# Gates kept as logits, an ungated attention projection, and another spacing of the attention's steps in a hybrid decoder block

## Chip, cores and metric

The kernel runs on one core of one Trainium2 chip. The metric is the device time of one execution in microseconds; the median of several executions is given.

## What is computed

One decoder block over 2048 tokens of width 1024, all in float32. A normalised input is projected to 7680 columns, and two branches run beside each other: a gated depthwise convolution over 31 taps with layernorm, and sliding-window attention (16 heads over 4 key-value heads, window 128, one sink a head). Each has a SiLU gate of its own, an output projection, and a sigmoid gate by which the two are merged.

```python
h = rmsnorm(x, norm_g[l])
proj = jnp.einsum("bsd,de->bse", h, w_in[l])
glu_in, conv_gate, q, k, v, attn_gate, merge_logits = jnp.split(proj, SPLIT_POINTS, axis=-1)
c = conformer_conv(glu_in, conv_dw_w[l], conv_dw_b[l], conv_ln_g[l], conv_ln_b[l])
y_conv = jnp.einsum("bsc,cd->bsd", c * jax.nn.silu(conv_gate), w_conv_out[l])
...
a = sliding_window_attention(q, k, v, attn_sinks[l])
y_attn = jnp.einsum("bsa,ad->bsd", a * jax.nn.silu(attn_gate), w_attn_out[l])
gates = jax.nn.sigmoid(merge_logits)
g_conv, g_attn = jnp.split(gates, 2, axis=-1)
merged = g_conv * y_conv + g_attn * y_attn
x = x + jnp.einsum("bsd,de->bse", merged, w_out[l])
return rmsnorm(x, final_norm_g)
```

## The kernel before

The tokens are taken in two sweeps of 1024. In a sweep nothing is transposed back: projections come out with 128 columns of weights on the partitions and 1024 tokens beside them, as two halves of 512. Every such item has 48 matmuls of 128x128 on 128x512, since each float32 operand is split into a high and a low part and three products are made (hi·hi, hi·lo, lo·hi). TensorE's order is the order of the code. The other engines' orders are made by a scheduler that takes instructions by readiness and priority.

The items of a sweep, in this order: k, v and q with rope (tiles ra, rb, hq); 32 gate items, ag (attention's gate), cg (convolution's gate), ma and mc (the two merge gates); among all these 8 pairs of items gb and ga (the convolution's input), each of which starts a convolution on VectorE (L513 and L520, 31 steps into acc, then cv); then ya, the attention's output projection, 8 items; yc, the convolution's, 8 items; and o, the last projection, 16 items.

A gate's values go from PSUM through an activation to a buffer of the ring t2k (five buffers of 128x512) and by DMA to HBM. They come back by `load_gate` where they are multiplied: cg with the layernormed convolution, giving u (`gated`, L927), ma in ya's evacuation (L999, into mp), mc in yc's (L1022, and GpSimd adds mp in L1023, giving mT by a split).

A clock of nominal microseconds, `Line`, places smaller work between the matmuls. It counts 3 x 0.2275 for three matmuls. `late` holds chains with a due time: a chain is a generator that yields the time its matmuls take and the time until its next step. `soon` holds single operations, one of which goes out at each count, and `bg` a queue of operations at a fixed interval, above all the convolutions' steps.

The attention is such a set of chains, 32 units a sweep (4 key-value heads, 8 blocks of 128 queries), one started each ATT_EVERY = 13.8, while the gate items run. A unit has three steps on TensorE: the scores (sc, eight small matmuls, L766); after LAT[0] four transposes of the softmax (tpp, L796); after LAT[1] the product with v (ov, six matmuls, L820). Between sc and tpp stand ScalarE's copy, VectorE's masked copy (L782) and maximum (L785), four exponentials (L787), a reciprocal and four scalings (L791). Between tpp and ov stand ScalarE's copy (L805) and VectorE's split (L253) into pt, and GpSimd's selection (L809) into pc. Behind ov come ScalarE's copies (L828) and VectorE's adds (L830), the gate (L831) and a split, and the result is stored to HBM, from where ya's operand aT is loaded. The scores of two halves, tpp and ov take turns in three PSUM banks (pool tp_ps). The projections have three banks of their own (mm_ps).

`high_priority(offset)` moves instructions ahead by so many places for the scheduler: 60 for an evacuation (PRIO), 120 for a step of a chain, 1200 where `front()` stands.

The pieces of q are stored to HBM by `drain`, a chain that issues one store each 2.0; `flush` issues what is left, before the buffers are used again and before the attention starts. SP, one queue, issues all DMAs, the weights' among them (L267 the raw weight; L270 its low part, kept in HBM by sweep 0 for sweep 1; L728 and L732 a unit's q and k).

Of the kernel before, what the change touches and what calls it, by code (L numbers as in the profile page):

```python
# [15 lines left out]
AF = mybir.ActivationFunctionType  # L16
ALU = mybir.AluOpType
# [5 lines left out]
KC = D // P  # L23
# [3 lines left out]
TH = 512  # L27
# [6 lines left out]
C_GLU_A, C_GLU_B, C_CGATE, C_Q, C_K, C_V, C_AGATE, C_MC, C_MA = (  # L34
    0, 1024, 2048, 3072, 4096, 4352, 4608, 5632, 6656)
# [9 lines left out]
ROPE_EVERY = 3.2  # L45
CONV_EVERY = 2.4
ATT_EVERY = 13.8
LAT = (27.0, 7.0)
PRIO = 60
SCALE = HD ** -0.5  # L50

# [2 lines left out]
def hybrid_block(ctx: ExitStack, tc: tile.TileContext, x, xt, par_d, w_in, w_conv, sinks, w_attn, w_out,  # L54
                 fin_g, rope_t, out):
    nc = tc.nc
    pe, act, dve, pool = nc.tensor, nc.scalar, nc.vector, nc.gpsimd
# [13 lines left out]
    def f(ap):  # L71
        return ap.bitcast(F32)
# [8 lines left out]
    def slot(tag, shape, dt, name):  # L81
        n = int(np.prod(shape[1:]))
        full = 1024 + P if tag in WIDE else 1024
        t = slots.tile([P, full], dt, tag=tag, name=name)
        v = t[:, 0:n]
        if len(shape) == 3:
            v = v.rearrange("p (a b) -> p a b", b=shape[2])
        elif len(shape) == 4:
            v = v.rearrange("p (a b c) -> p a b c", b=shape[2], c=shape[3])
        return v  # L90

    def t2k(name, dt=F32):
        return work.tile([P, TH], dt, tag="t2k", name=name, bufs=5)
# [75 lines left out]
    class Line:  # L169
# [27 lines left out]

        def step(self, chain, ok):

            with tc.high_priority(offset=2 * PRIO):  # L200
                got = next(chain, None)
            if got is not None:
                self.t += got[0]
                self.late.append((self.t + got[1], chain, ok))
# [40 lines left out]
    line = Line()  # L245
# [77 lines left out]
    def put_split(dst, src32, lo_eng):  # L323
        act.copy(dst[:, 0, :], src32)
        split_lo(dst[:, 1, :], src32, dst[:, 0, :], lo_eng)
# [171 lines left out]
    def sweep(s):  # L497
# [61 lines left out]
        def gate_item(kind, col, func, e):  # L559
            def ev(half, ps):  # L560
                g = t2k(f"{kind}{s}_{e}_{half}")
                act.activation(out=g, in_=ps, func=func)

                def store():
                    nc.sync.dma_start(out=spill[kind][s * KC + e, :, half * TH:(half + 1) * TH], in_=g)
                    if half == 1:
                        stored.add((kind, e))

                line.soon.append(store)

            return project(w_in[col // P + e], h_rhs, f"{kind}{s}_{e}", ev)

        def load_gate(kind, e, half):
            g = t2k(f"l{kind}{s}_{e}_{half}")
            nc.sync.dma_start(out=g, in_=spill[kind][s * KC + e, :, half * TH:(half + 1) * TH])
            return g


# [31 lines left out]
            t0 = s * T + half * TH  # L610
            nc.sync.dma_start(out=d_k[:, i, :, t0:t0 + TH].rearrange("a p t -> p a t"), in_=f(hl))

        pair, pend = {}, deque()

        def drain():
            while pend:
                pend.popleft()()
                yield 0.0, 2.0

        def flush():  # L620
            while pend:
                pend.popleft()()

        def store_q(r):
            def store(i, half, src):
                n = 2 * i + half
                if r % 2 == 0:
                    flush()
                    pair[n] = [slot(tags[n], [P, NB, 2, HD], F32R, f"hq{s}_{r}_{n}_{tags[n]}")
                               for tags in (AT[7:11], C[2:6])]  # L630
                hi, lo = (t[:, :, r % 2, :] for t in pair[n])
                src = src.rearrange("p (b t) -> p b t", t=HD)
                act.activation(out=hi, in_=src, func=AF.Copy, scale=SCALE)
                dve.scalar_tensor_tensor(out=lo, in0=src, scalar=SCALE, in1=f(hi), op0=ALU.mult,
                                         op1=ALU.subtract)
                if r % 2:
                    b0 = s * 2 * NB + NB * half
                    idle = not pend
                    for a in range(2):
                        pend.append(lambda a=a: nc.sync.dma_start(  # L640
                            out=d_q[a, i, :, b0:b0 + NB, r // 2, :],
                            in_=f(pair[n][a]).rearrange("p b h t -> p b (h t)")))
                    if idle:
                        line.start(drain())

            return store
# [104 lines left out]
        def attention(n):  # L751
# [38 lines left out]
            for h in range(GQ):  # L790
                act.activation(out=sb[:, h, :], in_=sb[:, h, :], func=AF.Copy, scale=rinv[:, h:h + 1])  # L791
            yield 0.90, LAT[0]

# [13 lines left out]
            for a in range(2):  # L807
                at = slice(a * HD, (a + 1) * HD)
                pool.affine_select(out=pc[at], in_=f(pt[0:HD, a]), pattern=[[0, 2 * GQ], [1, HD]],  # L809
                                   compare_op=ALU.is_ge, fill=0.0, base=0, channel_multiplier=-1)  # L810
            yield 0.44, LAT[1]

# [110 lines left out]
        aT, uT = [[None] * KC, [None] * KC], []  # L923

        def gated(dst, kind, e, half, other):
            g = load_gate(kind, e, half)
            dve.tensor_tensor(out=g, in0=g, in1=other(), op=ALU.mult)  # L927
            put_split(dst, g, dve)

# [25 lines left out]
            uT.extend(make_tiles(HT, h, f"uT{s}_") for h in range(2))  # L955

        gates = [gate_item("ag", C_AGATE, AF.Silu, e) for e in range(KC)]
        gates += [gate_item("cg", C_CGATE, AF.Silu, e) for e in range(KC)]
        gates += [gate_item("ma", C_MA, AF.Sigmoid, e) for e in range(KC)]
        gates += [gate_item("mc", C_MC, AF.Sigmoid, e) for e in range(KC)]  # L960
        line.every = ROPE_EVERY

        def ahead(item, work):
# [27 lines left out]
        mp = {}  # L991

        def ya_item(e, first):
            def ev(half, ps):
                if half == 0:
                    line.until(lambda: ("u", e, 1) in stored)
                    mp[e] = slot(C[e], [P, T], F32, f"mp{s}_{e}")
                g = load_gate("ma", e, half)
                dve.tensor_tensor(out=mp[e][:, half * TH:(half + 1) * TH], in0=ps, in1=g, op=ALU.mult)  # L999

            prefetch, blocks, _ = project(w_attn[e], lambda k, half: aT[half][k],
                                       f"ya{s}_{e}", ev)
            if not first:
                return prefetch, blocks

            def first_blocks():
                start_u()
                if None in aT[0] + aT[1]:
                    line.finish()
                yield from blocks()  # L1010

            return prefetch, first_blocks
# [4 lines left out]
        def yc_item(e):  # L1017
            def ev(half, ps):
                if not mT:
                    mT.extend(make_tiles(AT, h, f"mT{s}_") for h in range(2))  # L1020
                g = load_gate("mc", e, half)
                dve.tensor_tensor(out=g, in0=ps, in1=g, op=ALU.mult)  # L1022
                pool.tensor_tensor(out=g, in0=g, in1=mp[e][:, half * TH:(half + 1) * TH], op=ALU.add)  # L1023
                put_split(mT[half][e], g, dve)

            return project(w_conv[e], lambda k, half: uT[half][k], f"yc{s}_{e}", ev)
# [191 lines left out]
```

## Time and profile before

| | |
|---|---|
| median of 3 runs | 2040.08 us (2039.16 to 2041.83) |
| the profiled execution | 2039.39 us, of which the span is 2037.7 us |
| granted clock, mean | 0.995 |
| TensorE busy | 1989.0 us, 9264 matmuls |
| VectorE, ScalarE, GpSimd busy | 1312.7, 1002.2, 431.0 us |

The span runs from the first to the last instruction. Busy time of TensorE counts matmuls that overlap once, and a stalled or half-clocked matmul counts as busy too. In a row of a timeline stand start, duration, engine, line, operation, tiles written and read, the number of merged instructions, and in brackets how long the engine was idle and what ended that.

### The profile page before, as it was taken

Reading aid. Unit: us, or ns where it says so; the run is one execution under the profiler, and the core shown is the slowest. Engines: PE = TensorE matmul, PEld = TensorE weight load, DVE = VectorE, ACT = ScalarE, POOL = GpSimd, SP = SyncE. Lnnn points to the kernel's source line nnn. Section 1 sums busy time; section 2 is a strip of 40 time slices with the busy share of each in tenths; the row PEclk is TensorE's granted clock in tenths of the full one; section 3 lists DMA queues with packets and bytes.
Section 4 is the critical chain, followed back from the end, with each engine's and each line's share of the span. In section 5 each row is a group of like instructions: output and inputs, shape, how many; then the busy total and the mean of one; then the engine's idle time right before and its main releaser. Section 6 shows DMA issues by size and latency. Waiting matters only on the chain.

```text
span 2037.7 us, 27935 instructions
## 1 busy us (share of the span) xinstructions
PE 1989.0 (98%) x9264; PEld 1658.1 (81%) x9264; DVE 1312.7 (64%) x1737; ACT 1002.2 (49%) x2193; POOL 431.0 (21%) x462
## 2 busy tenths in 40 slices
PE   8999999999999999999999989999999999999998
PEld 7888888878787888888888878887888788888887
DVE  7999769878984176123857758688878824441324
ACT  7322576567667454123523125776666674621222
POOL 0444233233333222241011020111111110001200
PEclk9999999999999999999999999999999999999999
DMA  8655665555566857445647564565556578574432
GB/s 302 211 166 194 214 188 168 180 179 177 163 190 205 262 188 240 140 160 207 217 144 228 176 184 148 180 191 173 174 181 192 178 222 271 178 232 149 147 117 83
DMA packets 302785, 382.04 MB, mean 187 GB/s; under 512 B 30000, under 2 KB 160944, under 8 KB 302640
## 3 DMA queue, kind: packets, MB, share of 16 engines
q1 hardware_dynamic: 302640, 380.25, 57.5%
q8 instruction: 74, 1.21, 0.2%
q14 instruction: 71, 0.58, 0.1%
HBM read 252.20 MB, written 127.93 MB: 187 GB/s over the span
## 4 chain that ended last, share of the span: by engine, by line
PE 56%; DVE 20%; ACT 6%; issue 5%; DMA 2%; POOL 2%; SPq 1%; POOLq 0%; ACTq 0%; DVEq 0%
DVE acc L520 12%; PE o L1140 9%; PE mm_yc L291 9%; PE mm_mc L291 8%; PE mm_ya L291 7%; PE mm_ga L291 6%; PE mm_ma L291 5%; PE mm_gb L291 3%; PE mm_cg L291 2%; PE mm_ag L291 1%; ACT ss L787 1%; DVE st L785 1%; PE mm_q_a L291 1%; PE mm_v L291 1%; ACT L787 1%
## 5 line engine op out<-in xcount | busy, mean ns | idle before, releaser
L520 DVE SCALAR_TENSOR_TENSOR acc<-glu,par,acc 128x1024 f32<-128x1024 f32 x464 | 596.2, 1285 | 7.6
L1140 PE MATMUL o<-wo,mT 128*128 128x512 f32 x768 | 174.8, 389 | 0.0
L1140 PEld LDWEIGHTS o<-wo,mT 128*128 128x128 f32 x768 | 144.1, 188 | 30.0
L291 PE MATMUL mm_ma<-hT,whi_ma 128*128 128x512 f32 x512 | 160.8, 395 | 0.0
L291 PE MATMUL mm_cg<-hT,whi_cg 128*128 128x512 f32 x512 | 159.6, 393 | 0.0
L291 PE MATMUL mm_ag<-hT,whi_ag 128*128 128x512 f32 x512 | 159.6, 393 | 0.0
L291 PE MATMUL mm_mc<-hT,whi_mc 128*128 128x512 f32 x512 | 158.4, 390 | 0.0
L291 PE MATMUL mm_ya<-aT,whi_ya 128*128 128x512 f32 x512 | 157.6, 389 | 0.5 <-DVE mp L999 0.5
L291 PE MATMUL mm_yc<-uT,whi_yc 128*128 128x512 f32 x512 | 157.4, 389 | 0.0
L787 ACT ACT_TABLE_LOAD x61 | 78.3, 1283 | 148.3 <-DVE st L785 148.2
L809 POOL TENSOR_SCALAR_AFFINE_SELECT pc<-pt 64x512 fp32r<-64x512 f32 x128 | 84.5, 660 | 272.1 <-ACT pt L805 229.8
L291 PE MATMUL mm_ga<-hT,whi_ga 128*128 128x512 f32 x448 | 141.6, 398 | 0.0
L291 PE MATMUL mm_gb<-hT,whi_gb 128*128 128x512 f32 x448 | 140.1, 394 | 0.3 <-DVE rb_q__1_1662 L598 0.3
L830 DVE TENSOR_TENSOR ss<-ov,ss 64x256 f32<-64x256 f32 x128 | 53.8, 420 | 116.0 <-ACT ss L828 114.5
L291 PEld LDWEIGHTS mm_ya<-aT,whi_ya 128*128 128x128 f32 x512 | 96.0, 188 | 20.7 <-DVE mp L999 0.9
L291 PEld LDWEIGHTS mm_yc<-uT,whi_yc 128*128 128x128 f32 x512 | 96.1, 188 | 19.9
L291 PEld LDWEIGHTS mm_mc<-hT,whi_mc 128*128 128x128 f32 x512 | 95.4, 188 | 19.4
L291 PEld LDWEIGHTS mm_ma<-hT,whi_ma 128*128 128x128 f32 x512 | 94.8, 189 | 18.6
L291 PEld LDWEIGHTS mm_ag<-hT,whi_ag 128*128 128x128 f32 x512 | 94.5, 188 | 18.4
L291 PEld LDWEIGHTS mm_cg<-hT,whi_cg 128*128 128x128 f32 x512 | 93.9, 188 | 18.0
L787 ACT ACTIVATE ss<-ss,st 128x129 f32<-128x129 f32 x256 | 100.2, 394 | 16.9 <-DVE st L785 16.1
L291 PE MATMUL mm_ma<-hT,wlo_ma 128*128 128x512 f32 x256 | 100.4, 392 | 0.0
(445 smaller groups left out, 4296.1 us busy)
## 6 DMA issues: line engine op xcount, KB each, us to landing
qk<-d_q SPq DMA_DIRECT2D x256, 64.0 KB, 2.6
d_a<-ss SPq DMA_DIRECT2D x128, 128.0 KB, 2.6
aT<-d_a SPq DMA_DIRECT2D x32, 512.0 KB, 5.8
qk<-d_k SPq DMA_DIRECT2D x240, 64.0 KB, 2.1
d_q<-hq_c SPq DMA_DIRECT2D x16, 512.0 KB, 4.9
raw_ag<-in_w_in_dram SPq DMA_DIRECT2D x32, 256.0 KB, 3.4
d_ag<-ag SPq DMA_DIRECT2D x32, 256.0 KB, 2.2
pc<-d_ag SPq DMA_DIRECT2D x64, 128.0 KB, 2.7
```

Source lines behind the costliest of these rows:

```text
L291: pe.matmul(out=ps, lhsT=a, rhs=b, start=(k == 0 and i == 0), stop=(k == KC - 1 and i == 2))
L520: dve.scalar_tensor_tensor(out=to, in0=glu[c][:, j:j + T], scalar=tap(c, j), in1=acc[c], op0=ALU.mult, op1=ALU.add)
L785: dve.tensor_reduce(out=ngm, in_=ext, axis=AX.X, op=ALU.max, negate=True)
L787: act.activation(out=ext[:, h, :], in_=ext[:, h, :], func=AF.Exp, bias=ngm[:, h:h + 1], accum_out=den[:, h:h + 1])
L809: pool.affine_select(out=pc[at], in_=f(pt[0:HD, a]), pattern=[[0, 2 * GQ], [1, HD]], compare_op=ALU.is_ge, fill=0.0, base=0, channel_multi ...
L830: dve.tensor_tensor(out=to[r], in0=ovp[rows[r][0], :, r], in1=to[r], op=ALU.add)
L1140: pe.matmul(out=ps, lhsT=a[:, c0:c0 + P], rhs=r, start=(k == 0 and i == 0), stop=(k == KC - 1 and i == 2))
```

## The change

cg, ma and mc are stored as they come from the projection (a copy), and `load_gate` activates them in place, behind the load. ya's evacuation becomes a copy by ScalarE; yc's loads both merge gates, VectorE multiplies mp by ma's gate there, and GpSimd adds. LAT goes from (27, 7) to (19, 16), a step's priority from 120 to 1200 places. `drain` waits 4.0 before its first store, and then hands the stores to `soon`.

```diff
-LAT = (27.0, 7.0)
+LAT = (19.0, 16.0)
...
-            with tc.high_priority(offset=2 * PRIO):
+            with tc.high_priority(offset=20 * PRIO):
                 got = next(chain, None)
...
-                act.activation(out=g, in_=ps, func=func)
+                if func is None:
+                    act.copy(g, ps)
+                else:
+                    act.activation(out=g, in_=ps, func=func)
...
-        def load_gate(kind, e, half):
+        def load_gate(kind, func, e, half):
             g = t2k(f"l{kind}{s}_{e}_{half}")
             nc.sync.dma_start(out=g, in_=spill[kind][s * KC + e, :, half * TH:(half + 1) * TH])
+            act.activation(out=g, in_=g, func=func)
             return g
...
         def drain():
+            draining[0] = True
+            yield 0.0, 4.0
             while pend:
-                pend.popleft()()
+                line.soon.append(pend.popleft())
                 yield 0.0, 2.0
+            draining[0] = False
 
         def flush():
-            while pend:
-                pend.popleft()()
+            for ops in (line.soon, pend):
+                while ops:
+                    ops.popleft()()
...
-                    idle = not pend
+                    idle = not draining[0]
...
-            g = load_gate(kind, e, half)
+            g = load_gate(kind, AF.Silu, e, half)
...
-        gates += [gate_item("cg", C_CGATE, AF.Silu, e) for e in range(KC)]
-        gates += [gate_item("ma", C_MA, AF.Sigmoid, e) for e in range(KC)]
-        gates += [gate_item("mc", C_MC, AF.Sigmoid, e) for e in range(KC)]
+        gates += [gate_item("cg", C_CGATE, None, e) for e in range(KC)]
+        gates += [gate_item("ma", C_MA, None, e) for e in range(KC)]
+        gates += [gate_item("mc", C_MC, None, e) for e in range(KC)]
...
-                g = load_gate("ma", e, half)
-                dve.tensor_tensor(out=mp[e][:, half * TH:(half + 1) * TH], in0=ps, in1=g, op=ALU.mult)
+                act.copy(mp[e][:, half * TH:(half + 1) * TH], ps)
...
-                g = load_gate("mc", e, half)
+                ga, g = (load_gate(kind, AF.Sigmoid, e, half) for kind in ("ma", "mc"))
+                dve.tensor_tensor(out=ga, in0=mp[e][:, half * TH:(half + 1) * TH], in1=ga, op=ALU.mult)
                 dve.tensor_tensor(out=g, in0=ps, in1=g, op=ALU.mult)
-                pool.tensor_tensor(out=g, in0=g, in1=mp[e][:, half * TH:(half + 1) * TH], op=ALU.add)
+                pool.tensor_tensor(out=g, in0=g, in1=ga, op=ALU.add)
                 put_split(mT[half][e], g, dve)
```

What this makes of the engines' orders is seen at three places. The lines of the changed kernel are 8 further down from `drain` on (L766 is L774 there, L796 L804, L820 L828, L830 L838, L728 L736), 3 before it. A name is tile, sweep's own numbers (head and block for the attention) and a buffer number.

The first is TensorE in sweep 0, late in the attention. Before, the scores of unit 3_3 were followed at once by the transposes of unit 3_1, two units older:

```order
L291 MATMUL mm_ma_30_5734<-hT_0_4_456,whi_ma_31_5585 128x512 x2
L291 MATMUL mm_ma_30_5734<-hT_0_4_456,wlo_ma_31_5586 128x512
L766 MATMUL sc_3_3_0_5762<-qk_27_5607 128x192 x4
L766 MATMUL sc_3_3_1_5767<-qk_27_5607 128x192 x4
L796 MATMUL tpp_3_1_5790<-ident_r,ss_3_1_5477 128x128 x4
L291 MATMUL mm_ma_30_5734<-hT_0_5_457,whi_ma_31_5585 128x512 x2
L291 MATMUL mm_ma_30_5734<-hT_0_5_457,wlo_ma_31_5586 128x512
```

Now the same scores are followed by 24 matmuls of the gate, and then by the transposes of unit 3_2, one unit older, with ov of unit 3_1 another 12 matmuls behind:

```order
L804 MATMUL tpp_3_2_5830<-ident_r,ss_3_2_5638 128x128 x4
L291 MATMUL mm_ma_31_5815<-hT_1_4_543,whi_ma_31_5598 128x512 x2
L291 MATMUL mm_ma_31_5815<-hT_1_4_543,wlo_ma_31_5599 128x512
L291 MATMUL mm_ma_31_5815<-hT_1_5_544,whi_ma_31_5598 128x512 x2
L291 MATMUL mm_ma_31_5815<-hT_1_5_544,wlo_ma_31_5599 128x512
L291 MATMUL mm_ma_31_5815<-hT_1_6_545,whi_ma_31_5598 128x512 x2
L291 MATMUL mm_ma_31_5815<-hT_1_6_545,wlo_ma_31_5599 128x512
L291 MATMUL mm_ma_31_5815<-hT_1_7_546,whi_ma_31_5598 128x512 x2
L291 MATMUL mm_ma_31_5815<-hT_1_7_546,wlo_ma_31_5599 128x512
L828 MATMUL ov_3_1_5859<-pt_3_1_5695,vt_0_716 128x256 x2
```

So tpp and ov of one unit moved apart, and sc and tpp of one unit together.

The second is VectorE at the same place, in the last convolution of sweep 0 (acc_7). Before, seven of its steps stood between the split of pt of unit 3_1 and that unit's adds:

```order
L253 TENSOR_TENSOR pt_3_1_5797<-tpp_3_1_5790,pt_3_1_5797 128x512
L785 TENSOR_REDUCE st_3_3_5778<-ss_3_3_5772 128x4
L520 SCALAR_TENSOR_TENSOR acc_7_5977<-glu_7_5255,par,acc_7_5977 128x1024 x3
L789 RECIPROCAL st_3_3_5778<-st_3_3_5778 128x4
L520 SCALAR_TENSOR_TENSOR acc_7_5977<-glu_7_5255,par,acc_7_5977 128x1024 x4
L830 TENSOR_TENSOR ss_3_1_5477<-ov_3_1_5847,ss_3_1_5477 64x256 x2
```

Now the split of the next unit's pt comes first, behind the reciprocal and one step:

```order
L793 TENSOR_REDUCE st_3_3_5785<-ss_3_3_5779 128x4
L520 SCALAR_TENSOR_TENSOR acc_7_5986<-glu_7_5267,par,acc_7_5986 128x1024 x2
L797 RECIPROCAL st_3_3_5785<-st_3_3_5785 128x4
L520 SCALAR_TENSOR_TENSOR acc_7_5986<-glu_7_5267,par,acc_7_5986 128x1024
L253 TENSOR_TENSOR pt_3_2_5837<-tpp_3_2_5830,pt_3_2_5837 128x512
L520 SCALAR_TENSOR_TENSOR acc_7_5986<-glu_7_5267,par,acc_7_5986 128x1024 x2
L838 TENSOR_TENSOR ss_3_1_5490<-ov_3_1_5859,ss_3_1_5490 64x256 x2
```

The convolution's steps are as many as before, and stand between other instructions of the attention.

The third is SP in sweep 1, where the attention starts. Before, the last of eight stores of q (hq), a unit's q and k and then the two halves of the weight wlo_ga:

```order
L640 DMA d_q<-hq_2_3_a_10418 128x8x128
L640 DMA d_q<-hq_2_3_c_10419 128x8x128
L728 DMA qk_0_10651<-d_q 32x512 x4
L732 DMA qk_0_10651<-d_k 32x2x256 x3
L270 DMA wlo_ga_20_10583<-d_lo 128x512
L270 DMA wlo_ga_21_10589<-d_lo 128x512
```

Now the weight's halves stand among the stores, and five stores come later:

```order
L648 DMA d_q<-hq_2_0_h_10438 128x8x128
L270 DMA wlo_ga_20_10644<-d_lo 128x512
L740 DMA qk_1_10828<-d_k 32x2x256 x2
L648 DMA d_q<-hq_2_3_a_10482 128x8x128
L648 DMA d_q<-hq_2_3_c_10483 128x8x128
L736 DMA qk_0_10715<-d_q 32x512
L736 DMA qk_1_10828<-d_q 32x512
L740 DMA qk_1_10828<-d_k 32x2x256 x2
L270 DMA wlo_ga_21_10650<-d_lo 128x512
L648 DMA d_q<-hq_2_0_c_10439 128x8x128
```

The weight moved ahead of most of the stores of q.

More of the change, by code (lines that the diff above doesn't have):

```diff
@@ L611, in store_k @@
             nc.sync.dma_start(out=d_k[:, i, :, t0:t0 + TH].rearrange("a p t -> p a t"), in_=f(hl))
-        pair, pend = {}, deque()
+        pair, pend, draining = {}, deque(), [False]
         def drain():
+            draining[0] = True
+            yield 0.0, 4.0
             while pend:
-                pend.popleft()()
+                line.soon.append(pend.popleft())
                 yield 0.0, 2.0
+            draining[0] = False
         def flush():
-            while pend:
-                pend.popleft()()
+            for ops in (line.soon, pend):
+                while ops:
+                    ops.popleft()()
         def store_q(r):
```

## The prediction

> **What bounds the kernel now.** I read the page first: who is busy, and what the chain that ended last is made of.
>
> ```profile
> span 2037.7 us, 27935 instructions
> PE 1989.0 (98%) x9264; PEld 1658.1 (81%) x9264; DVE 1312.7 (64%) x1737; ACT 1002.2 (49%) x2193; POOL 431.0 (21%) x462
> ...
> PE 56%; DVE 20%; ACT 6%; issue 5%; DMA 2%; POOL 2%; SPq 1%; POOLq 0%; ACTq 0%; DVEq 0%
> ```
>
> TensorE (PE) is the bound, and the change leaves its 9264 matmuls alone; it moves some among each other. So the change is worth what it does to TensorE's idle time and to its clock, and nothing else. VectorE (DVE) holds a fifth of the chain, so it must be what TensorE waits for in places. The view of waits, for PE alone, says which:
>
> ```profile
> PE tpp L796 <- DVE ss L830: 19.7, 21, 3.1
> PE ov L820 <- POOL pc L809: 7.9, 7, 2.2
> PE mm_gb L291 <- ACT u_c L361: 5.5, 1, 5.5
> PE mm_ga L291 <- DMA wlo_ga<-d_lo: 5.4, 1, 5.4
> PE tpp L796 <- ACT ss L791: 1.1, 2, 0.8
> PE mm_q_b L291 <- DMA wlo_q_b<-d_lo: 0.8, 1, 0.8
> PE ov L820 <- DVE pt L253: 0.6, 1, 0.6
> PE mm_ya L291 <- DVE mp L999: 0.5, 1, 0.5
> ```
>
> The columns are total, times, longest. The transposes of the softmax (tpp) and the product with v (ov) wait 19.7 + 7.9 + 1.1 + 0.6 = 29.3 us over 64 attention units. One weight at the start of sweep 1's gates costs 5.4. The 5.5 at mm_gb is the kernel's opening, which stays. After four of these waits the granted clock fell to a half; these are windows laid on those stretches (length, then PE, PEld, DVE, ACT and POOL busy, granted clock, DMA share, GB/s):
>
> ```profile
> 338.71:342.13 3.42, 3.42 (x10) 2.66 (x10) 3.39 (x6) 2.27 (x6) 0.76 (x2) 0.50 0.69 218
> 618.61:622.02 3.41, 3.41 (x10) 2.63 (x9) 3.41 (x4) 1.16 (x3) 1.73 (x1) 0.50 0.39 113
> 1212.53:1219.35 6.82, 4.85 (x11) 3.84 (x12) 0.00 (x0) 0.00 (x0) 0.00 (x0) 0.50 0.80 232
> 1424.15:1427.57 3.42, 3.42 (x10) 2.65 (x9) 0.50 (x2) 3.36 (x9) 0.00 (x0) 0.50 0.46 130
> ```
>
> At half clock, half of the busy time is lost: 3 x 3.42 / 2 = 5.1 us in the attention, and 4.85 / 2 = 2.4 at the weight. All that the change can win is thus 29.3 + 5.4 + 5.1 + 2.4 = 42.2 us, with 1.3 more at q_b and ya.
>
> **The spacing (LAT).** How long a place in TensorE's queue is from another, I count in matmuls:
>
> ```profile
> 1020.72 10.88 PE mm_gb L291 x48
> ```
>
> One costs 10.88 / 48 = 0.227 us. Before, tpp of unit n stood right behind the scores of unit n+2, and 33 matmuls (with its own, 7.9 us) ahead of ov of unit n; from that ov to the next tpp were 5.7 us. Small results share three PSUM banks in turn, so a tpp needs the bank of the ov just before it: 5.7 us for ScalarE's copies (L828) and VectorE's adds (L830). Now tpp of unit n+1 stands 24 matmuls (6.3 us with the scores) behind the scores of n+2, and ov of unit n 12 matmuls further. A unit's period without waits is about 13.65 us (some 51 projection matmuls, 11.6, and about 2.1 for its own 18 small ones), so the new distances are: ov to the tpp that takes its bank 10.5 us (was 5.7); tpp to its own ov 13.65 + 3.1 = 16.8 (was 7.9); scores to their tpp 13.65 + 6.3 = 19.9 (was 28); and tpp to the second scores that take its bank 7.8 (was 13.2). Two distances grow, two shrink.
>
> The shrunk one of the softmax has a worst case in the unit whose scores start at 540.47:
>
> ```profile
> 540.47 1.03 PE L766 MATMUL sc<-qk 128*128 128x192 f32 x8
> ...
> 557.17 1.28 ACT L791 ACTIVATE ss<-ss,st 128x128 f32<-128x128 f32 x4
> ```
>
> That is 18.0 us from the scores' start to the last scaling, inside 19.9, and I found none longer among the 64. GpSimd's pc, which ov waited for, gets 16.8 us where 7.9 fell short by 2.2 at most. What is late next is the other shrunk one: the bank of tpp, freed by VectorE's split of pt (L253). It hangs on VectorE's lag in a convolution, seen best in the last one of sweep 0:
>
> ```profile
> 569.39 0.39 PE L291 MATMUL mm_ga<-hT,wlo_ga 128*128 128x512 f32 x1
> 570.10 0.69 DVE L547 TENSOR_TENSOR glu<-mm_ga,glu 128x512 f32<-128x512 f32 x1
> ...
> 578.83 5.26 DVE L520 SCALAR_TENSOR_TENSOR acc<-glu,par,acc 128x1024 f32<-128x1024 f32 x4
> ...
> 608.52 0.38 PE L820 MATMUL ov<-pc,va 128*128 128x256 f32 x1 [0.59 <-POOL pc L809]
> 613.23 1.03 PE L766 MATMUL sc<-qk 128*128 128x192 f32 x8
> 616.40 0.85 DVE L830 TENSOR_TENSOR ss<-ov,ss 64x256 f32<-64x256 f32 x2
> 617.39 0.63 PE L796 MATMUL tpp<-ident_r,ss 128*128 128x128 f32 x4 [3.13 <-DVE ss L830]
> ```
>
> When the gate's multiply (L547) frees a convolution, its 31 steps of 1.29 us stand in VectorE's queue between the attention's, ten to a unit: 12.9 us, and with the unit's own eleven instructions that is more than the period. The lag grows from unit to unit until the convolution ends. From 570.10 to 617.25 VectorE works without a pause, 47.2 us, and TensorE pays the 3.13. In the new order, fewer steps stand ahead of the split that counts: from L547 to the third pt split 25 convolution steps instead of 28 up to that L830, and one pair of L830 (0.85) less, so 47.2 - 3 x 1.29 - 0.85 = 42.5 us, ending at 612.6 on this clock. The second half of these scores starts at 613.23 + 0.45 = 613.7, less the wait of 0.59 ahead of it that goes: 613.1. That is a tie within one convolution step, where before TensorE lost more than 3 us. The same count for all twelve convolutions gives 24.6 us of lateness before, against 20.8 measured at tpp, and 8.9 after, 3.5 of it in the first units of sweep 1. I take 7 us of new waits, at sc. The ends are 0 (each tie holds) and 21 (VectorE's lateness stays as it is, and only changes its place).
>
> **Priority, logits, activations.** With 20 instead of 2 times 60 for each step, a unit's instructions move ahead of evacuations and convolution steps in the queues of ScalarE, VectorE and SP. TensorE's projections have three banks, so an evacuation may come two halves, 2 x 24 x 0.227 = 10.9 us, late; a unit's ScalarE work is far below that. I cost it at nothing; if that cover went, a step of 0.6 us would show for each evacuation. A unit's DMAs move with it, but ss lives as long as before (ov stands 36.7 us behind its scores, 36 before) against the four periods, 54.6, until its buffer is wanted. The activations:
>
> ```profile
> L787 ACT ACT_TABLE_LOAD x61 | 78.3, 1283 | 148.3 <-DVE st L785 148.2
> L562 ACT ACT_TABLE_LOAD x55 | 70.6, 1283 | 3.1 <-DMA d_mc<-mc 1.5 <-issue 0.7
> L562 ACT ACTIVATE cg<-mm_cg 128x512 f32<-128x512 f32 x32 | 19.2, 598 | 0.4
> ```
>
> The order shows 31 and 17 table loads on these two lines, 68 fewer: 87 us of ScalarE. What is added is 96 activations at the load and 32 copies of ya, 128 x 0.6 = 77 us. ScalarE is at half load, so neither is on the path by itself; the shorter softmax is a help that I leave in the tie above.
>
> **ya and yc.** In sweep 0 the u steps (L927, now with a Silu ahead) stand between the normalisation and ya's copies.
>
> ```profile
> 757.61 0.61 PE L291 MATMUL mm_ya<-aT,whi_ya 128*128 128x512 f32 x2
> 760.06 6.92 ACT L896 ACTIVATE cv<-cv,par 128x1024 f32<-128x1024 f32 x6
> ```
>
> Down ScalarE's new order from 760.06 to the weights of ya's third item, with 1.15 for an apply and 0.6 for the rest, I count 18 us, 778.4, and 1.3 for GpSimd's low half; TensorE gets there at 757.6 + 96 x 0.227 = 779.4. That is another tie: the 0.5 of mp goes, and I put 1 us there, between 0 and one half, 5.4. In yc each half now loads two gates into a ring of five buffers, so the load for half i+2 waits for GpSimd's add of half i:
>
> ```profile
> L1022 DVE TENSOR_TENSOR lmc<-mm_yc,lmc 128x512 f32<-128x512 f32 x32 | 22.1, 691 | 53.5 <-PE mm_yc L291 53.5
> L1023 POOL TENSOR_TENSOR lmc<-lmc,mp 128x512 f32<-128x512 f32 x32 | 42.0, 1311 | 258.7 <-DVE lmc L1022 258.7
> lmc<-d_mc SPq DMA_DIRECT2D x32, 256.0 KB, 2.6
> ```
>
> 0.69 + 1.31 + 2.6 + 0.6 = 5.2 us against two halves of 5.44 each: hidden, with 5.7 to spare. SP's queue carries the weights behind those waiting loads, but they stand an item ahead.
>
> **The stores of q.** In sweep 1 the weight wlo_ga stood in SP's queue behind eight stores of q and the loads of qk that need them:
>
> ```profile
> 1208.46 0.61 PE L291 MATMUL mm_ga<-hT,whi_ga 128*128 128x512 f32 x2
> ...
> 1205.86 1.21 SPq L640 DMA_DIRECT2D d_q<-hq_c  x1
> 1207.12 2.71 SPq L728 DMA_DIRECT2D qk<-d_q  x4
> 1209.87 1.36 SPq L732 DMA_DIRECT2D qk<-d_k  x3
> 1211.33 0.85 SPq L270 DMA_DIRECT2D wlo_ga<-d_lo  x2
> ...
> 1214.50 0.80 PE L291 MATMUL mm_ga<-hT,wlo_ga 128*128 128x512 f32 x1 [5.43 <-DMA wlo_ga<-d_lo]
> ```
>
> In the new order its first part stands behind one store alone, and its second behind two more stores and six loads of qk, at about 1206.5 (the last store of the trace issues at 1205.86, and a load costs 0.45). TensorE needs that part 12 matmuls into the item, 2.7 us after 1208.46. With the 3.1 us that the rows show from issue to start it is in time by more than 1 us, so 5.4 + 2.4 = 7.8 us go. The other end is that none go.
>
> **The sum.** 2037.7 - 29.3 - 5.1 - 7.8 + 7 + 0.5 = 2003.0 us of span. The profiled execution took 2039.39, 1.7 above its span, and stands 0.7 below the median of 2040.08; so 2003.0 + 1.7 + 0.7, about 2005 us.
>
> The clock term rests on the four windows: no wait of the attention was longer than 3.1 us, and three of them were followed by 3.4 us at half clock. [...]
>
> **Rivals.** *The lag only changes its place.* For it: VectorE's work in a convolution is the same, and pt's distance shrank from 13.2 to 7.8. Against: the count above, and VectorE's average, 64%. It decides once pt is split more than 7.8 us after its tpp in most convolutions. Then 21 instead of 7 us of waits, and the clock falls as before: 2005 + 14 + 5 = 2024.
> *SP's order doesn't help.* One store that lands late holds the weight all the same: 2005 + 7.8 = 2013.
> *The clock halves whatever the waits.* For it: of the attention's 31 waits only three were followed by half clock, so a wait alone doesn't make it. Against: none of the four windows lies where TensorE had not just waited. Then the 5.1 us stay: 2010.
> *Slower: yc becomes bound by its ring.* If the chain from add to sigmoid takes 14 us instead of 5.2, two halves last 14 instead of 10.9, and 32 halves lose 1.55 each: 50 us, 2055. It costs from 10.9 on, and turns the whole slower from 13.1 on (35 us over 32 halves). For it: SP serves the loads in order, and they wait. Against: 5.7 us to spare.
> *The change does nothing that counts*: waits of other kinds fill the place of those gone, 2040.
>
> **How the numbers follow.** The forecast, with the ties within some us of 2005 (1997 to 2012), has 0.57; the moved lag 0.14; SP's order 0.11; the clock 0.09; yc 0.05; nothing 0.04. The range from 1996 (no new waits, 2005 - 7, and a little for q_b and ya) to 2022 takes in all but the moved lag's upper part and the last two. A difference of 0.2%, 4 us, is about what can be told from none. All but the last two cases are faster by more: 0.91; same 0.04; slower 0.05.
>
> **What would show it.** In the profile after, tpp's and ov's rows among PE's waits should be gone or under 3 us together, a new row should name sc and VectorE's pt with 3 to 12 us, wlo_ga should be absent, and no 3.4 us stretch in the attention at clock 0.50. Table loads should fall from 145 to 77. It is wrong if sc's row is above 20, if yc or ya appear among the waits with more than 5 us, or if a weight's DMA does.

## The result, and the profile after

The changed kernel takes 2026.2 us (median of four executions, 2024.4 to 2027.9) against 2039.8 us for the kernel before: a ratio of 0.9932, 95% interval 0.9914 to 0.9949. It is faster, but by 13.5 us and not by the 35 that the forecast gave; the forecast of 2005 and its whole range, up to 2022, lie below it.

The head of the page of the changed kernel (its profiled execution took 2025.4 us):

```profile
span 2023.7 us, 27913 instructions
PE 1989.0 (98%) x9264; PEld 1656.4 (82%) x9264; DVE 1302.1 (64%) x1737; ACT 976.3 (48%) x2253; POOL 430.2 (21%) x462
...
PE 64%; DVE 16%; ACT 5%; issue 4%; DMA 1%; POOL 0%; SPq 0%; ACTq 0%; DVEq 0%; POOLq 0%
```

TensorE holds more of the chain than before (64% against 56%) and VectorE less (16 against 20). The waits of TensorE, columns total, times, longest (left out: the kernel's opening, 5.5 as before):

```profile
PE sc L774 <- DVE pt L253: 10.4, 13, 1.6
...
PE mm_q_b L291 <- DMA wlo_q_b<-d_lo: 4.4, 1, 4.4
PE mm_ag L291 <- DMA wlo_ag<-d_lo: 3.6, 1, 3.6
PE sc L774 <- issue: 2.9, 1, 2.9
```

tpp and ov, 29.3 us before, are gone, and so is wlo_ga's 5.4. In their place stand 10.4 us of sc behind VectorE's split of pt, and three single stalls that no term of the forecast has: two low weights of sweep 1 (one of them, q_b's, stood at 0.8 before) and the first scores of sweep 0. Windows laid on the stretches at half clock (length, then PE, PEld, DVE, ACT, POOL busy, granted clock, DMA share, GB/s):

```profile
211.16:217.98 6.82, 6.49 (x19) 5.50 (x20) 1.47 (x4) 4.49 (x14) 0.70 (x1) 0.50 0.90 280
412.54:415.96 3.42, 3.42 (x11) 2.74 (x11) 3.34 (x5) 0.91 (x2) 1.61 (x2) 0.50 0.74 236
1098.62:1102.04 3.42, 3.42 (x10) 2.66 (x9) 0.43 (x1) 0.00 (x0) 0.00 (x0) 0.50 0.62 225
1221.50:1224.92 3.42, 3.42 (x10) 2.64 (x9) 3.26 (x5) 1.78 (x4) 0.00 (x0) 0.50 1.00 347
```

Three of the four follow the three stalls; one (412.54) follows a wait of sc. In both kernels the clock is at a half once more in the last 2 to 4 us of the span, where no matmul is left and it costs nothing (from 2035.14 and 2020.22 on; the last matmuls end at 2031.1 and 2016.8). The table loads fell as forecast, from 145 to 77; these are the two largest groups:

```profile
L795 ACT ACT_TABLE_LOAD x31 | 39.8, 1283 | 59.2 <-DVE st L793 59.1
L565 ACT ACT_TABLE_LOAD x17 | 21.8, 1283 | 0.3
```

Why the three stalls? SP's queue shows it. First q_b in sweep 1, SP's rows (start, length of issue), then TensorE's:

```profile
1075.65 0.33 SPq L270 DMA_DIRECT2D wlo_q_b<-d_lo  x1
...
1089.65 2.05 SPq L685 DMA_DIRECT2D d_v<-vt  x2
...
1094.43 0.55 SPq L270 DMA_DIRECT2D wlo_q_b<-d_lo  x1
```

```profile
1097.69 0.50 PE L291 MATMUL mm_q_b<-hT,wlo_q_b 128*128 128x512 f32 x1 [4.37 <-DMA wlo_q_b<-d_lo]
```

In the kernel before, the two parts of this weight were issued 4.6 us apart (1084.24 and 1088.83). Now v's stores and v's loads, which wait for those stores, stand between: the second part is issued 18.8 us after the first, and arrives 3.2 us later. They got there by the step's priority, since v's transposes are such a step (v_item), and the DMAs they issue move with it. At the first scores of sweep 0:

```profile
200.44 3.20 SPq L736 DMA_DIRECT2D qk<-d_q  x5
203.68 1.83 SPq L740 DMA_DIRECT2D qk<-d_k  x4
...
206.65 0.62 SPq L648 DMA_DIRECT2D d_q<-hq_a  x1
208.74 0.79 SPq L736 DMA_DIRECT2D qk<-d_q  x2
```

```profile
211.49 1.94 PE L774 MATMUL sc<-qk 128*128 128x64 f32 x8 [2.94 <-issue]
```

One of the two loads at 208.74 is the last piece of unit 0's q; the store it needs, at 206.65, now goes out behind seven loads of unit 1. The profile names no releaser and calls the wait "issue". It ends 2.75 us after the first of these two loads goes out, and the page's median from issue to landing of such a load is 2.6; that the load is what the scores wait for is inferred from this, and tested below. The weight of ag is the same once more: behind the last two stores of q, which stand behind six loads.

```profile
1209.56 5.07 SPq L736 DMA_DIRECT2D qk<-d_q  x6
...
1215.14 0.58 SPq L648 DMA_DIRECT2D d_q<-hq_c  x1
1215.82 1.98 SPq L270 DMA_DIRECT2D wlo_ag<-d_lo  x2
```

### The profile page after: what moved, and what is told of

The parts are those of the page before. It is cut to its first block, busy times and chain, and to the rows that moved or that the text cites. A ratio compares the mean times of both kernels' runs of the same rounds, so it can differ in the third digit from the quotient of the medians.

```text
span 2023.7 us, 27913 instructions
## 1 busy us (share of the span) xinstructions
PE 1989.0 (98%) x9264; PEld 1656.4 (82%) x9264; DVE 1302.1 (64%) x1737; ACT 976.3 (48%) x2253; POOL 430.2 (21%) x462
## 4 chain that ended last, share of the span: by engine, by line
PE 64%; DVE 16%; ACT 5%; issue 4%; DMA 1%; POOL 0%; SPq 0%; ACTq 0%; DVEq 0%; POOLq 0%
DVE acc L520 10%; PE mm_mc L291 9%; PE o L1148 9%; PE mm_ya L291 9%; PE mm_yc L291 9%; PE mm_ma L291 6%; PE mm_ag L291 5%; PE mm_ga L291 5%; PE mm_gb L291 4%; PE mm_q_a L291 2%; PE mm_q_b L291 2%; PE sc L774 1%; ACT ss L795 1%; DVE st L793 1%; PE mm_v L291 1%
## 5 line engine op out<-in xcount | busy, mean ns | idle before, releaser
L291 PE MATMUL mm_ag<-hT,wlo_ag 128*128 128x512 f32 x256 | 100.6, 393 | 3.6 <-DMA wlo_ag<-d_lo 3.6
L291 PE MATMUL mm_cg<-hT,wlo_cg 128*128 128x512 f32 x256 | 100.0, 391 | 0.0
```

The lines of the kernel that those rows point to most:

```text
L291: pe.matmul(out=ps, lhsT=a, rhs=b, start=(k == 0 and i == 0), stop=(k == KC - 1 and i == 2))
```

## The experiments

Line numbers in their rows are those of each kernel, a few off from the changed kernel's.

### Which part makes the three stalls

One part undone at a time: the step's priority, the stores of q, both.

```diff
-            with tc.high_priority(offset=20 * PRIO):
+            with tc.high_priority(offset=2 * PRIO):
...
-            draining[0] = True
-            yield 0.0, 4.0
             while pend:
-                line.soon.append(pend.popleft())
+                pend.popleft()()
                 yield 0.0, 2.0
...
-                    idle = not draining[0]
+                    idle = not pend
```

> The changed kernel with one part undone: a step's priority is 2 x 60 again (L200). In the changed kernel's trace three stalls are not explained by the forecast's sum: the low part of q_b in sweep 1 (4.5 us and 1.5 at half clock), the low part of ag (3.8 + 1.6) and the first scores of sweep 0 (3.1 + 3.0). Theory A, the place in SP's queue: the priority put v's loads, which wait for v's stores, ahead of wlo_q_b. With it undone the order has wlo_q_b two rows ahead of those loads, so its 6.0 us go and nothing else: 2026.2 - 6.0 = 2020. ag and the first scores stay, because the stores' part is untouched. Rival B, the stall only moves: another transfer is late by as much, 2026. Rival C, the priority is what keeps the softmax inside its spacing: sc's 10.4 us grow and tpp comes back, 2026 or more.

> The changed kernel with one part undone: the stores of q are issued as before (drain, flush and the idle test). Theory A: the new way of issuing them put unit 0's last load of q behind seven loads of unit 1, and wlo_ag behind the last two stores and six loads; undone, the first scores (3.1 + 3.0) and ag (3.8 + 1.6) start in time, but wlo_ga stands behind eight stores and the loads of two units again, 8 us or somewhat more than before's 5.6 + 2.4, and q_b keeps its 6.0, which belong to the priority: 2026.2 - 11.5 + 8 to 10 = 2023 to 2025. Rival B, these stalls come from the priority, not from the stores: the first scores and ag stay, and ga's 8 come on top, 2034. Rival D: the waits at sc behind pt depend on how the stores are placed: sc's row changes from 10.4.

> The changed kernel with the priority and the stores of q both as before; the spacing and the logits stay. Theory A, the terms of the two parts add: q_b's 6.0, ag's 5.4 and the first scores' 6.1 go, ga's 8.0 come back as in the kernel before, sc's waits of 10.4 + 1.7 stay: 2026.2 - 17.5 + 8.0 = 2016.7. Rival C, without the priority the softmax no longer holds its spacing: sc and tpp wait more than 12 us together, 2022 or more.

Measured: priority undone 2019.5 us (2019.0 to 2019.6), stores undone 2032.9 (2030.9 to 2034.4), both 2020.3 (2019.9 to 2023.4). The waits of TensorE that differ, of the kernel with the priority undone:

```profile
PE sc L774 <- DVE pt L253: 13.4, 17, 1.7
PE sc L774 <- issue: 2.9, 1, 2.9
PE mm_ag L291 <- DMA wlo_ag<-d_lo: 1.1, 1, 1.1
```

with the stores undone:

```profile
PE mm_ga L291 <- DMA wlo_ga<-d_lo: 7.7, 1, 7.7
PE mm_q_b L291 <- DMA wlo_q_b<-d_lo: 6.9, 2, 5.1
```

and with both undone:

```profile
PE sc L770 <- DVE pt L253: 13.6, 16, 1.7
PE mm_ga L291 <- DMA wlo_ga<-d_lo: 4.9, 1, 4.9
PE mm_q_b L291 <- DMA wlo_q_b<-d_lo: 1.7, 1, 1.7
```

So q_b's stall is the priority's: it goes with it, and the kernel is 6.7 us faster without that part of the change. That theory A's 6.0 came out so well is in part luck: it left ag and sc as they were, but ag's wait fell by 2.5 and the half clock behind it went, while sc's waits rose by 3.0. The first scores' stall is the stores': the row is there with the priority undone and absent in both others. ag needs both: 3.6 with the two, 1.1 with the new stores alone, none with the old ones. But the old stores bring wlo_ga's stall back, and more of it with the high priority (7.7) than without (4.9); that is why undoing the stores alone makes the kernel slower, 8 us beyond theory A's 2023 to 2025. There A had the right places and mis-sized them: q_b waits 6.9 and not 4.4, sc 12.0 and not 10.4, and three stretches at half clock stand in the attention (407.72, 1339.56, 1554.59) where A left one. Rival B's 2034 is nearer in time, but the rows that it kept, the first scores and ag, are gone.

With both undone the terms don't add up either: 2020.3 us against 2016.7 from A. sc waits 3.2 more than A had it, and 1.7 of q_b stay. Rival C's sign came (sc above 12), its 2022 did not. Whether the priority helps the softmax at all stays open: sc waits 13.4 and 13.6 without it, and 10.4 and 12.0 with it, but two runs further down have it the other way, 12.1 without and 13.8 with it. tpp never waits in any of these.

### What the spacing is worth, and what the logits are

```diff
-LAT = (27.0, 7.0)
+LAT = (19.0, 16.0)
```

That is the spacing alone, in the kernel before. The logits alone are the changed kernel with LAT, priority and stores as before, and in that kernel the table loads are put back by

```diff
-                if func is None:
-                    act.copy(g, ps)
-                else:
-                    act.activation(out=g, in_=ps, func=func)
+                act.activation(out=g, in_=ps, func={"ag": AF.Silu, "cg": AF.Silu}.get(kind, AF.Sigmoid))
```

> The kernel before with the spacing alone (LAT 19 and 16); its 145 table loads stay. Theory A, the whole gain is the spacing's and the logits cost and bring nothing to TensorE: tpp's and ov's 29.3 us and 5.1 at half clock go, sc's waits of about 12 come: 2039.8 - 34.4 + 12 = 2017.5, equal to the run with priority and stores undone within 2 us. Rival E, the logits carry part of it: the softmax of a unit with its table loads of 1.28 us ends later, which shows as tpp behind ScalarE or as a larger row of sc behind pt, 2022 to 2030.

> The kernel before with the logits alone (gates stored as logits, activated where used, ya kept ungated); spacing, priority and stores of q as before. It closes the square of spacing and logits: neither 2039.3, spacing alone 2031.0, both 2020.3. Theory F: the logits help by 1.28 us of table load less inside a unit's softmax, and matter only where the softmax's end is near; in the old spacing its end had more than 13 us to spare, so tpp and ov wait for the banks as before, 25 to 29 us, and the time is 2034 to 2040. Rival G: the logits' 10.7 us of the other row of the square are ScalarE's load, which is lighter whatever the spacing: 2028 to 2030.

> The run with the logits alone (2023.5), with the table loads put back: cg, ma and mc are evacuated through Silu and Sigmoid as in the kernel before, and activated a second time where they are used, so the output is not the reference's; ya stays ungated, yc keeps its two loads. 147 table loads instead of 77, 145 in the kernel before. Theory T, the logits' 15.6 us come from ScalarE's table loads in the attention, which delay its copies of pt and ov: tpp's row returns to about 20 us, ov's to 8, two more stretches at half clock return, and the time to 2036 to 2041. Rival U, the gain lies in the rest of the edit (ya and yc, the apply steps): 2022 to 2026.

| priority and stores as before | LAT 27, 7 | LAT 19, 16 |
|---|---|---|
| gates activated when stored | 2039.2 | 2031.0 |
| logits | 2023.5 | 2020.3 |
| logits, table loads put back | 2038.1 | |

Ratios to the kernel before: 0.9956 (0.9944 to 0.9969) for the spacing alone, 0.9925 (0.9911 to 0.9938) for the logits alone, 0.9994 (0.9985 to 1.0003) with the loads put back. Theory A fell (2017.5 forecast). What keeps the spacing alone from it is sc, 16.8 and not about 12, and four stretches in the attention at half clock (378.66, 409.38, 1334.39, 1477.75), where A had none. Rival E's larger row of sc came, at a time just beyond its 2030. F fell (2034 to 2040), and G was too high as well (2028 to 2030). The logits alone bring 15.6 us, and 14.6 of them are lost again with the table loads, as T said, though only one of its two further stretches at half clock returned (618.64). The rest of that edit brings nothing that shows. With the logits in, the spacing adds 3.2. The rows, of the spacing alone, of the logits alone, and of the logits with the loads put back:

```profile
PE sc L766 <- DVE pt L253: 16.8, 13, 2.5
```

```profile
PE tpp L800 <- DVE ss L834: 14.9, 16, 2.1
PE ov L824 <- POOL pc L813: 3.5, 4, 1.4
```

```profile
PE tpp L797 <- DVE ss L831: 20.0, 21, 3.3
PE ov L821 <- POOL pc L810: 6.9, 7, 2.3
```

How 1.28 us of ScalarE reach TensorE through a row that names VectorE is seen in one unit, VectorE's, ScalarE's and TensorE's rows of the kernel before:

```profile
475.90 0.68 DVE L785 TENSOR_REDUCE st<-ss 128x4 f32<-128x516 f32 x1
...
480.56 2.53 DVE L520 SCALAR_TENSOR_TENSOR acc<-glu,par,acc 128x1024 f32<-128x1024 f32 x2
483.00 0.85 DVE L830 TENSOR_TENSOR ss<-ov,ss 64x256 f32<-64x256 f32 x2
```

```profile
476.66 1.28 ACT L787 ACT_TABLE_LOAD   x1 [2.69 <-DVE st L785]
...
479.63 1.28 ACT L562 ACT_TABLE_LOAD   x1
...
481.55 0.75 ACT L828 COPY ss<-ov 64x256 f32<-64x256 f32 x2
```

```profile
483.99 0.63 PE L796 MATMUL tpp<-ident_r,ss 128*128 128x128 f32 x4 [1.65 <-DVE ss L830]
```

and VectorE's of the same unit in the kernel with the logits alone:

```profile
473.97 0.69 DVE L789 TENSOR_REDUCE st<-ss 128x4 f32<-128x516 f32 x1
...
478.60 1.23 DVE L520 SCALAR_TENSOR_TENSOR acc<-glu,par,acc 128x1024 f32<-128x1024 f32 x1
479.74 0.85 DVE L834 TENSOR_TENSOR ss<-ov,ss 64x256 f32<-64x256 f32 x2
```

With cg activated at once, two table loads of 1.28 us stand on ScalarE, one ahead of the exponentials (L787) and one ahead of cg's Silu (L562), before it copies ov out of its bank: 2.6 us. With logits none stands there. VectorE's adds, which free the bank, start 7.1 us behind the reduction, against 5.8 with logits. TensorE's tpp waits 1.65 us for them; with logits this unit's tpp does not wait for them at all. VectorE is not idle in between: five steps of the convolution stand between the reduction and the adds before, four with logits. The loads thus show in the order of VectorE's instructions, which is made anew for each kernel by readiness, and not as a wait of VectorE; whether they would also delay the adds in an order that is kept was not tested. The row of TensorE's wait names the last link, VectorE; ScalarE's loads are two links before it. Between the kernels with 77 and with 147 loads lie 14.6 us.

### The weights first in SP's queue

If the place in the queue is the cause, a weight that is put ahead is in time. One line, in the kernel with both parts undone and in the changed kernel with the stores undone:

```diff
-                nc.sync.dma_start(out=f(lo), in_=d_lo[at, kh])
+                with tc.high_priority(offset=40 * PRIO):
+                    nc.sync.dma_start(out=f(lo), in_=d_lo[at, kh])
```

> The kernel with spacing and logits, priority and stores of q as before, and one line new: the load of a stored low part of a weight gets a priority of 40 x 60, which puts wlo_q_b and wlo_ga ahead of v's and qk's waiting loads in SP's queue. Theory A, the place in the queue is all that makes these weights late: ga's 4.9 us, q_b's 1.7 and ga's half clock of 1.7 go, 2020.3 - 8.3 = 2012. Rival B, the stall moves: the loads of qk, now behind the weights, make the first scores late by 3 to 6 us, 2015 to 2020.

> The changed kernel with the stores of q issued as before and the same new line for the low weights; the step's priority stays 20 x 60. Theory A: of the run with the stores undone (2032.9), ga's 7.7 us with 5.1 at half clock and q_b's 6.9 with 1.9 and more at half clock go, so 2032.9 - 12.8 - 9 = 2011, the same as without the priority within 2 us. Then the forecast's 2005 lacks only what it mis-sized at sc. Rival H, a high step priority costs in other places too: 2016 or more.

Measured: 2012.7 us (2012.4 to 2013.4) and 2013.3 (2011.5 to 2015.1). No low weight is left among the waits of either; 1.8 us for the high part of ag's weight are new. Theory A holds within 2.5 us, and with it that the high priority, once the weights are ahead, costs nothing that shows. Then, in the first of the two, the spacing by its two numbers alone (17 and 18, 18 and 17), and at 17 and 18 the high part:

```diff
-LAT = (19.0, 16.0)
+LAT = (17.0, 18.0)
...
-            nc.sync.dma_start(out=raw, in_=src[:, 4 * kh:4 * kh + 4, :])
+            with tc.high_priority(offset=40 * PRIO):
+                nc.sync.dma_start(out=raw, in_=src[:, 4 * kh:4 * kh + 4, :])
```

> As the run with the new line for the low weights (priority and stores of q as before), with LAT 17 and 18 instead of 19 and 16: tpp stands six matmuls (1.4 us) nearer to its scores, ov stays where it is. Theory I, sc waits because tpp and the second scores that take its bank stand 7.8 us apart: 9.2 us end all of the waits of sc behind pt but 1 or 2 us (of 13.6, none longer than 1.9), while the next tpp, now 9.1 us behind the ov whose bank it takes, waits 1 to 4: some 10 us below the run without this, near 2002. Rival J, VectorE's lag only changes its place again: tpp behind the adds or the softmax waits 10 us or more, 2010 or above.

> The run with the new line for the low weights and LAT 17 and 18 (2006.0), with 18 and 17: tpp stands on the average one step of two to four matmuls later. In the two neighbours sc waits 12.1 us with the next bank 7.8 us away, and tpp 7.8 us with its bank 9.1 us behind ov. Theory I, the two distances trade against each other and the waits are ties of some tenths each: halfway both rows are smaller than half of their sum, 3 to 6 us together instead of 8.9, and the time 2002 to 2005. Rival J, the waits only move: 9 to 11 us together, 2006 to 2009.

> The run with LAT 17 and 18 (2006.0), with the same priority of 40 x 60 for the load of a weight's high part too, which ScalarE's copy waits for in ag's second item of sweep 1 (1.8 us there). In the order this load moves from behind qk's loads of three units to ahead of them. Theory A, the place in the queue makes it late: 1.8 us less, 2004. Rival B, the loads of qk move behind it and the first scores or units are late instead: 2006 to 2010.

Waits of sc and tpp at LAT 19 and 16, at 18 and 17, and at 17 and 18:

```profile
PE sc L771 <- DVE pt L253: 12.1, 16, 1.7
```

```profile
PE sc L771 <- DVE pt L253: 9.6, 11, 1.6
```

```profile
PE tpp L801 <- DVE ss L835: 7.8, 11, 1.5
PE sc L771 <- DVE pt L253: 1.1, 2, 0.7
```

2012.7, 2008.8 and 2006.0 us. For 17 and 18 neither theory holds as priced (near 2002, and 2010 or above). The waits of sc and tpp shrink from 12.1 to 9.8 us in all (0.9 of tpp stands in another row), which is not the whole of the 6.7 us gained; the busy time of the sc matmuls (128x192) falls too, from 66.1 to 62.6, and a stretch at half clock (407.24) is gone. At 18 and 17 the waits have only changed their place (rival J), and theory I's halfway optimum isn't there. 17 and 18 is the best kernel of this study, at 0.9836 of the kernel before (0.9823 to 0.9850). Putting the high parts ahead too was a mistake, 2033.5 us:

```profile
PE mm_gb L293 <- ACT u_c L363: 14.6, 2, 11.6
PE sc L772 <- DMA qk<-d_k: 11.4, 2, 6.6
```

The second row is the first scores of each sweep. A raw weight waits for a free buffer (SP stands still 14 times, 32.1 us in all, until GpSimd has split an earlier part of ag), and the loads of the first units' q and k now stand behind that wait; with both the clock falls to a half (from 222.50 and from 1222.61 on). This is rival B, far above the 2006 to 2010 it was priced at. The first row, 5.6 us without this edit, is the kernel's opening, which neither theory had: eight loads of raw weights now go out ahead of 11 of the input's 12 (xr_a), from which ScalarE makes u_c. The two rows make 20.4 of the 27.5 us.

### When the clock falls

Pauses of a chosen length, in the kernel with LAT 17 and 18:

```diff
+        def stall(n):
+            tp = tp_ps.tile([P, 4, P], F32, tag="tp", name=f"st{next(stalls)}")
+            pe.transpose(out=tp[:, 0, :], in_=ident, identity=ident)
+            for _ in range(n):
+                act.copy(pause, tp[:, 0, :])
+            pe.transpose(out=tp[:, 1, :], in_=pause, identity=ident)
```

> The run with LAT 17 and 18 and the new line for the low weights (2006.0, no half clock but at its end), with sixteen pauses of TensorE put into the last output projection, one in the middle of each block of 24 matmuls: a transpose, 1 to 8 copies on ScalarE one behind another (in the order 1, 4, 7, 2, 5, 8, 3, 6, twice), and a transpose that waits for the last copy. Its outputs are the same; the time is longer by the pauses, about 0.8 to 2.9 us each, 30 us in all. It measures when a pause is followed by half clock. Theory W, fixed windows: all stretches at 0.50 in ten traces begin on one grid of 3.413 us, and follow a window of that grid in which TensorE was idle 1.9 us or more; so here a pause of 2.0 us or more is followed by half clock only where 1.9 to 2.05 us of it lie in one window, which is so for about half of the six longest, and none below 1.9 us is: 3 or 4 stretches, 2036 + 6. Rival X, the length of the wait alone decides, from 1.8 us on: all six to eight of the longest are followed. Rival Y, only 3.4 us without a matmul count: none is.

Measured: 2048.3 us (2045.0 to 2049.1); the execution profiled took 2045.0 and has four stretches at half clock among the sixteen pauses. Two of the pauses (in brackets the wait), and two of the stretches:

```profile
1930.13 0.33 PE L1137 MATMUL st<-ident_r,pause 128*128 128x128 f32 x1 [2.20 <-ACT pause L1136]
...
1992.77 0.33 PE L1137 MATMUL st<-ident_r,pause 128*128 128x128 f32 x1 [2.20 <-ACT pause L1136]
```

```profile
1953.01:1956.42 3.41, 3.41 (x10) 2.66 (x9) 0.00 (x0) 0.00 (x0) 0.00 (x0) 0.50 0.00 0
1993.97:1997.38 3.41, 3.41 (x10) 2.66 (x9) 0.00 (x0) 0.00 (x0) 0.00 (x0) 0.50 0.00 0
```

The two stretches start 40.96 us apart, which is 12 times 3.413. Counted on that grid, the wait of 2.20 that ends at 1992.77 lies whole in the window from 1990.56 to 1993.97, and the next window runs at half clock. The equal wait that ends at 1930.13 has a window's end at 1929.12 in it, 1.2 us on one side and 1.0 on the other, and nothing follows. The four pauses that were followed have 2.2 us or more of wait in one window each; of the twelve others none has, the wait of 1.90 that ends at 2033.36 included. X and Y fall. Theory W holds in the grid and in the number of stretches; its time, 2042, was 3 us short of this execution and 6 of the median.

Its bound of 1.9 us does not hold. In the changed kernel the stretch at 412.54 follows this wait:

```profile
412.14 0.83 PE L774 MATMUL sc<-qk 128*128 128x192 f32 x4 [1.65 <-DVE pt L253]
```

It lies whole in one window (409.13 to 412.54), and TensorE has no other gap there. The equal wait of 1.65 us that ends at 483.99 in the kernel before, shown further up, lies whole in one window too (482.07 to 485.48), and no half clock follows. Counted like this in the kernels before and after, from the opening's end to the last matmul, all seven windows in which TensorE was idle for 1.97 to 3.41 us are followed by half clock, and of the six with 1.61 to 1.88 two are.

## Why the prediction was wrong

From the forecast's span of 2003.0 to the measured 2023.7, by the rows above (half of each stretch at half clock is counted as lost, an estimate from the granted clock of 0.50; behind the pauses the 24 matmuls lost 1.6 us of such a stretch's 3.41): q_b 4.4 - 0.8 + 3.42/2 = 5.3; ag 3.6 + 1.7 = 5.3; the first scores 2.9 + 6.49/2 = 6.1; sc 10.4 - 7 = 3.4; one stretch at half clock left in the attention, 1.7; less 1.0 at ya, where the 0.5 of before went and the 1 put in its place did not come. Sum 2023.8, against 2023.7.

**SP's queue: the step that failed.** "I cost it at nothing" (the priority) was wrong by q_b's 5.3, for it does more than move evacuations: it moves the DMAs of every step in SP's queue. Its cover was looked for in the evacuations and in the units' DMAs; v's chain, a step of the same kind, has stores and loads too, and a weight stood behind them. "In time by more than 1 us" (the stores of q) was right for wlo_ga, which was all that was asked. What else the new place delayed, unit 0's own q and the next weight behind wlo_ga, was not followed: 11.4 us. The rival that wlo_ga's stall stays, 2013, had the right engine and queue, but not the other items of that queue; with the weights put ahead, all the rest of the change except the stores' part took 2013.3, and of the 8.3 us that this lies above 2005 sc's row, 13.8 there instead of 7, makes 6.8 and ag's high part 1.8.

**The spacing: right in place, right in size by luck.** tpp's and ov's 29.3 us went, and the bank of tpp became the late one, as the count of VectorE's lag had it, at 10.4 us, between the forecast's ends of 0 and 21. But that size is the spacing's and the logits' together. With the spacing alone sc waits 16.8 us and the attention's clock falls four times, and it brings 8.3 us, not the 22 or so that 34.4 less 12 of waits would leave.

**Logits: costed at nothing, worth 15.6 alone.** "ScalarE is at half load, so neither is on the path by itself" is an average over stages. In the unit shown two loads stand on ScalarE between VectorE's reduction and the copies out of ov's bank. The total was not hurt, since spacing and logits remove the same waits (8.3 and 15.6 us alone, 19.0 together), but the credit stood in the wrong place.

**The clock.** The forecast had it that short waits lower it and that without them it stays up. Where the attention had three stretches one is left, in another place, and three new ones came with the stalls. Which waits are followed by half clock it could not say. The pauses show a part of it: the stretches behind them are 3.41 us long and start on one grid of 3.413. The stretches of the kernels before and after, up to the last matmul, agree with that, in length (3.41, 3.42 or 6.82) and in place (in the kernel before, 618.61, 1212.53 and 1424.15 are 82, 256 and 318 windows from 338.71). In the window ahead of a stretch TensorE was idle for 2.2 to 2.5 of the 3.41 us at the pauses, and for 1.65 at 412.14.

**Right:** tpp's, ov's and wlo_ga's rows gone, 77 table loads, no wait at ya or yc (the slower rival's ring costs nothing).

## What to carry to other kernels

Where a step gets another priority or place, list every DMA that any chain of that kind issues, and for each the item that stands right behind it in the queue; here SP's queue handed one item's wait to those behind it (the second part of wlo_q_b was issued 18.8 us after the first), and three late items cost more (16.7 us by the count above) than every tie in the attention together (10.4). A wait's row names only the last link, so follow it further back before the cost of another engine's instruction is called hidden. And where two parts of a change remove the same wait, only a square of runs tells what each is worth.

## What the runs showed of the hardware

In the kernels before and after and behind the pauses, the stretches at half clock up to the last matmul were 3.41 or 3.42 us long, or 6.82, and in each of these traces they started on one grid of 3.413 us. A pause of TensorE of 2.20 us within one window of that grid was followed by half clock in the next one, and the 24 matmuls behind it took 7.37 us; behind the equal pause with a window's end in it they took 5.72. So in one kernel the same wait was followed by half clock at one place in the grid and not at another. Place is not all: of two waits of 1.65 us, each whole within a window, one was followed and one was not, and the eleven pauses of 1.90 us and less never were. The first scores' wait of 2.94 us was followed by two windows at half clock (211.16 to 217.98), though TensorE was idle for only 0.33 us of the first of them. Whether the small matmuls around these waits count less in a window stays open.
